# One core: modulation sums issued a step later, and the last attention-output tiles with the router's top 64 by halves of the tokens

## Chip, cores and metric

One NeuronCore of a Trainium2 chip runs the whole program. The metric is the time of one execution on the device in microseconds (us), as the median over several runs. The engines are TensorE (PE, with its weight loads as PEld), VectorE (DVE), ScalarE (ACT), GpSimd (POOL) and SyncE (SP), whose queue issues most of the DMAs.

## What is computed

A hidden state x of 512 tokens by 1024 features goes through two layers (an mLSTM mixer and a short convolution, each followed by an MLP with squared ReLU) and then through a block with modulated norms, two kinds of attention and a mixture of 16 experts. All is float32. Cut to what the change touches:

```python
mod = einsum('bd,de->be', silu(c), w_mod) + b_mod        # 6 x 1024 values, from 1024 inputs
mod_c = einsum('d,de->e', silu(c_ctx), w_mod) + b_mod    # its first 2 x 1024 values are used
...
x = x + g_a * mix                                        # mix = [o_a, o_b] @ w_out
h2 = modulate(rmsnorm(x, norm_ffn), sh_f, sc_f)
x = x + g_f * ec_moe(h2, w_router, w_gate, w_up, w_down)

def ec_moe(h, w_router, w_gate, w_up, w_down):           # 512 tokens, 16 experts
    aff = softmax(einsum('bnd,de->bne', h, w_router), axis=-1)
    vals, idx = top_k(swapaxes(aff, 1, 2), 64)           # each expert takes its 64 best tokens
    # per expert: gather, silu(xs @ w_gate) * (xs @ w_up), @ w_down, times vals, scatter-add
```

## The kernel before

Activations are kept with features on the 128 partitions and tokens along the free dimension: `self.x[:, k]` is feature tile k (of 8), 512 tokens wide. Every GEMM (`gemm`, `mm3`, L92 to L94) is three fp32r matmuls per 128-deep step: high part of the weights with both parts of the activations, and the low part of the weights with their high part. A tile of 128 features by 512 tokens is thus 24 matmuls for a depth of 1024, and 12 for a depth of 512. Weights come as 1 MB pieces through SP's queue (`wpiece`). ACT makes the high half (L85, tag `wh`) and DVE the low half (L86, tag `wl`), two instructions of each per piece; during the MLPs there are four buffers of either, so two pieces.

The compiler orders each engine's instructions itself: the order of the code is their priority, and an instruction that is ready early can stand ahead of an earlier one. `keep_in_program_order` pins an instruction behind the one that precedes it in the code on the same engine. Within an engine instructions start in the order of its queue.

The modulation vector is computed inside the two MLPs by a generator, `mods`, which `mlp` advances (`next(filler)`, L701 and L711) once ahead of each `down(f)` and once behind it. `down(f)` is 8 tiles of 12 matmuls for one of eight blocks of hidden features; the products of a later block (4 tiles of 24, two weight pieces) come between two `down`s. For columns j of `w_mod` (24 blocks of 256) DVE multiplies rows of weights by the silu values and adds them up (L877 first, then L881, tiles `u`, weights `b`). For j under 8 there are two vectors, the token condition and the context's. The first sum of an even j is pinned (L879). `rows` (L842) then sums four such accumulators over the partitions with four matmuls of 32 columns of ones at four column positions of PE, and ACT copies the result (L845). `columns` (L852) transposes it, and DVE copies it to `mod` (L856, L858). In the code, the sums of a pair of blocks and `rows` stand together behind a `down(f)`, and `columns` ahead of the next one.

`attention_out` multiplies the attention result by `w_out`, tile k after tile k. Behind each tile's GEMM stands the router's part of the tile before it (`stats`, L1391): four matmuls with 128 tokens of x as weights and the router's 16 columns moving, eight records in the trace since float32 takes two. DVE updates x (L1409), ACT squares it (L194), and the squares are added on POOL or DVE (L196). Behind the last tile come the column sums of the squares (L207), the reciprocal root (`rstd_cols`, L156 to L162), and the scaled logits (L1415).

`route` computes the softmax (L1424 to L1431) and transposes the affinities to 16 rows of 512 tokens (L1434, L1436). Eight rounds of a maximum of eight (L1460) and a replacement by -1 (L1462) find each expert's top 64. What became negative is selected (L1467, L1469), and matmuls with triangular ones count ranks (L1471, L1473, L1476). Meanwhile PE transposes x to tokens and ACT writes it, scaled, to HBM (`h2d`, L1454 to L1456). One-hot matrices (L1489) give the slots (L1499), and POOL fetches each pair of experts' tokens by an indirect DMA (L1511). `moe` then runs the experts in pairs. The first 15 expert weight tiles are loaded ahead, behind the weights of `attention_out` in SP's queue; later ones wait until their buffers are free.

Of the kernel before, what the change touches and what calls it, by code (L numbers as in the profile page):

```python
# [18 lines left out]
S = 512  # L19
# [8 lines left out]
class Net:  # L28
# [42 lines left out]
    def sm(self, shape, dt=F32):  # L71
        self.n += 1
        return self.smp.tile(shape, dt, name=f"sm{self.n}", tag=f"sm{shape[-1]}", bufs=16 if shape[-1] <= 2 else 2 if shape[-1] == 64 else 8)
# [101 lines left out]
    class Sumsq:  # L175
# [7 lines left out]
        def add(self, src, sl=slice(0, S)):  # L183
# [9 lines left out]
            sq = net.t([128, S]) if lo + 2 == hi else net.t([128, 256], tag="th")  # L193
# [635 lines left out]
    def mods(self):  # L829
# [30 lines left out]
        sums = []  # L860
        for j in range(24):
# [20 lines left out]
            if j % 2:  # L882
                t = None
# [6 lines left out]
                yield  # L890
# [483 lines left out]
    def attention_out(self, oops):  # L1374
# [8 lines left out]
        wa = self.t([128, KD, 16], tag="wr")  # L1383
        nc.gpsimd.tensor_tensor(wa, wr, self.A[:, :, 2][:, :, None].to_broadcast([128, KD, 16]), op=OP.mult)
# [4 lines left out]
        def stats(k):  # L1389
            for c in range(4):  # L1390
                nc.tensor.matmul(pl[:, c * 16:c * 16 + 16], self.x[:, k, c * 128:c * 128 + 128], wa[:, k], start=k + c == 0,  # L1391
                                 stop=k == KD - 1 and c == 3, skip_group_check=True)

        for k in range(KD):
            j = (k + 1) // 2
            if k % 2 == 0 and j + 2 < 5:
# [12 lines left out]
            nc.vector.scalar_tensor_tensor(self.x[:, k], p, self.mod[:, 16 + k, 0:1], self.x[:, k], op0=OP.mult, op1=OP.add)  # L1409
            ss.add(self.x[:, k])  # L1410
        stats(KD - 1)
        cols, _ = self.colsum(ss.acc)
        lg = self.sm([128, 64])
        for c in range(4):
            nc.vector.scalar_tensor_tensor(lg[:, c * 16:c * 16 + 16], pl[:, c * 16:c * 16 + 16], cols[:, c:c + 1], shw,  # L1415
                                           op0=OP.mult, op1=OP.add)
        return cols, lg.rearrange("p (c e) -> p c e", c=4)

    def route(self, cols, lg):
        nc, a = self.nc, self.a  # L1420
        self.tok = self.t([128, S + 4], tag="tok")
        nc.scalar.dma_start(self.tok, a["k_tok"])
        mx = self.sm([128, 4])
        nc.vector.reduce_max(mx, lg, axis=AX.X)  # L1424
        nc.vector.tensor_tensor(lg, lg, mx[:, :, None].to_broadcast([128, 4, 16]), op=OP.subtract)
        nc.scalar.activation(lg, lg, AF.Exp)
        sm = self.sm([128, 4])
        nc.vector.reduce_sum(sm, lg, axis=AX.X)
        ri = self.sm([128, 4])
        nc.vector.reciprocal(ri, sm)  # L1430
        nc.vector.tensor_tensor(lg, lg, ri[:, :, None].to_broadcast([128, 4, 16]), op=OP.mult)  # L1431
        pT = self.p()
        for c in range(4):
            nc.tensor.transpose(pT[0:16, c * 128:(c + 1) * 128], lg[:, c], self.ident)  # L1434
        aT = self.t([16, S], tag="aT")
        nc.vector.tensor_copy(aT, pT[0:16])  # L1436
# [8 lines left out]
        nc.gpsimd.tensor_sub(self.mv[:, :, :, 3:6:2], l4, self.mv[:, :, :, 2:6:2].bitcast(F32))  # L1445

        self.h2d = self.tc.dram_tile([S, D], F32, name="h2d")
        hd = self.h2d.rearrange("(c p) d -> c p d", p=128)
        for c in range(4):
            t = self.t([128, D], tag="wh" if c else "ha")  # L1450
            for hf in range(2):
                p = self.p()
                for j in range(4):
                    nc.tensor.transpose(p[:, j * 128:(j + 1) * 128], self.x[:, hf * 4 + j, c * 128:(c + 1) * 128], self.ident)  # L1454
                nc.scalar.activation(t[:, hf * 512:hf * 512 + 512], p, AF.Copy, scale=cols[:, c:c + 1])
            nc.scalar.dma_start(hd[c], t)  # L1456
        wk = aT
        for r in range(8):
            v = self.sm([16, 8])
            nc.vector.max(v, wk)  # L1460
            nw = self.t([16, S], tag="aT")
            nc.vector.match_replace(out=nw, in_to_replace=v, in_values=wk, imm_value=-1.0)  # L1462
            wk = nw

        pT = self.p()
        for c in range(4):
            nc.tensor.transpose(pT[:, c * 16:c * 16 + 16], wk[:, c * 128:(c + 1) * 128], self.ident[0:16, 0:16])  # L1467
        sel = self.t([128, 4, 16], BF, tag="sel")
        nc.vector.tensor_scalar(sel, pT[:, 0:64].rearrange("p (c e) -> p c e", c=4), 0.0, None, op0=OP.is_lt)  # L1469
        pp = self.p()[:, 0:64].rearrange("p (c e) -> p c e", c=4)  # L1470
        nc.tensor.matmul(pp, tri[:, 0], sel, start=True, stop=False, skip_group_check=True)  # L1471
        for c in range(3):
            nc.tensor.matmul(pp[:, c + 1:], tri[:, 1], sel[:, c:c + 1].to_broadcast([128, 3 - c, 16]), start=False, stop=c == 2,  # L1473
# [315 lines left out]
```

## Time and profile before

| | before |
|---|---|
| median of 3 runs | 1856.34 us (1850.32 to 1859.35) |
| the profiled execution | 1856.87 us |
| its span in the trace | 1854.9 us, mean granted clock 0.975 |
| PE busy | 1753.0 us, 95% (weight loads 1364.1 us, 74%) |
| DVE busy | 1026.3 us, 55% |
| ACT busy | 676.8 us, 36% |
| POOL busy | 150.6 us, 8% |

Times are from the start of the span. Matmul records overlap: each has its full duration though the next starts before it ends, so the distance between starts tells the pace. PEclk is the granted share of TensorE's clock, 1.00 for 2.4 GHz and 0.50 for 1.2 GHz. "[7.52 <-DVE u L881]" behind an instruction is the idle time of its engine ahead of it and what ended it. In the chain of waits, each row is a step of the work that ended last. The timeline leaves out buffer numbers and joins neighbours of one kind ("x8").

### The profile page before, as it was taken

What the parts mean: (1) busy time and instruction counts of PE and PEld (TensorE: products, weight loads), DVE (VectorE), ACT (ScalarE), POOL (GpSimd) and SP (SyncE); (2) the same over time, 40 slices, a digit from 0 to 9 for tenths busy, and PEclk for the clock granted to TensorE, in tenths of its full rate; (3) what the DMA queues carried; (4) which work ended last, traced back from release to release, by engine and by line L of the source; (5) the groups of instructions that cost most, each with busy time, mean ns of one, the idle gap of its engine ahead of it and who ended that gap; (6) DMA issues with size and microseconds to landing.
All of it is one profiled execution on the core that took longest, in us unless ns stands there. A gap on an engine that the chain in (4) does not pass through costs nothing.

```text
span 1854.9 us, 24070 instructions
## 1 busy us (share of the span) xinstructions
PE 1753.0 (95%) x9629; PEld 1364.1 (74%) x9633; DVE 1026.3 (55%) x1953; ACT 676.8 (36%) x1220; POOL 150.6 (8%) x132
## 2 busy tenths in 40 slices
PE   7999999988899999999999999989989998799997
PEld 5798898766687888889787878888777787343334
DVE  4544673456665585537455554578777843342322
ACT  4444444322233253335333333345666642111112
POOL 1000000000000000000000001012334321000000
PEclk9899999988999999999999999989999999899999
DMA  6222423233443423322434432220100048799995
GB/s 191 69 69 65 153 80 114 91 113 114 136 137 114 136 86 97 114 91 92 137 113 137 136 117 91 91 73 12 24 12 9 20 144 305 255 390 393 394 390 185
DMA packets 193535, 254.45 MB, mean 137 GB/s; under 512 B 19975, under 2 KB 125840, under 8 KB 193296
## 3 DMA queue, kind: packets, MB, share of 16 engines
q1 hardware_dynamic: 188688, 244.70, 39.2%
q10 hardware_dynamic: 3232, 3.97, 0.7%
q0 software_dynamic: 1504, 4.26, 0.6%
q8 instruction: 75, 1.23, 0.3%
q14 instruction: 36, 0.29, 0.1%
HBM read 248.71 MB, written 4.19 MB: 136 GB/s over the span
## 4 chain that ended last, share of the span: by engine, by line
PE 84%; DVE 8%; ACT 3%; DMA 3%; issue 1%; POOL 1%; SPq 0%; DVEq 0%; ACTq 0%; POOLq 0%
PE ps L92 21%; PE ps L93 21%; PE ps L94 21%; PE ps L1595 5%; PE ps L1572 3%; PE ps L1187 2%; DMA mw<-in_w_up_dram 2%; PE ps L1172 2%; PE pw L1315 1%; DVE u L881 1%; PE ps L1564 1%; DMA wl<-h2d,slots 1%; DVE wl L86 1%; PE ps L1565 1%; PE ps L842 1%
## 5 line engine op out<-in xcount | busy, mean ns | idle before, releaser
L92 PE MATMUL ps<-op,wh 128*128 128x512 f32 (+1 forms) x1808 | 656.4, 368 | 7.3 <-ACT wh L85 2.3
L93 PE MATMUL ps<-op,wh 128*128 128x512 f32 (+1 forms) x1808 | 659.2, 366 | 0.8 <-DVE op L105 0.6
L94 PE MATMUL ps<-op,wl 128*128 128x512 f32 (+1 forms) x1808 | 657.2, 365 | 2.5 <-DVE wl L86 2.5
L86 DVE TENSOR_TENSOR wl<-raw,wh 128x1024 fp32r<-128x1024 f32 x210 | 258.2, 1233 | 276.9 <-ACT wh L85 276.4
L92 PEld LDWEIGHTS ps<-op,wh 128*128 128x128 f32 x1808 | 339.4, 190 | 71.8 <-issue 4.1
L94 PEld LDWEIGHTS ps<-op,wl 128*128 128x128 f32 x1808 | 342.2, 190 | 64.2 <-DVE wl L86 3.1
L93 PEld LDWEIGHTS ps<-op,wh 128*128 128x128 f32 x1808 | 342.7, 190 | 62.0 <-issue 1.8
L85 ACT CAST wh<-raw 128x1024 fp32r<-128x1024 f32 x210 | 219.9, 1052 | 382.3 <-PE ps L93 346.7
L688 DVE TENSOR_TENSOR t<-t,ps 128x512 f32<-128x512 f32 x96 | 65.8, 685 | 101.7 <-PE ps L94 101.6
L1595 PE MATMUL ps<-mw,xs 128*64 128x512 f32 x400 | 114.2, 607 | 3.1 <-DMA mw<-in_w_up_dram 3.1
L881 DVE SCALAR_TENSOR_TENSOR u<-b,csilu,u 128x256 f32<-128x256 f32 x224 | 103.9, 493 | 9.5 <-DMA b<-in_w_mod_dram 5.8
L196 POOL TENSOR_TENSOR acc<-acc,t 128x512 f32<-128x512 f32 x21 | 28.2, 1342 | 630.3 <-ACT t L194 629.7
L637 ACT ACTIVATE t<-ps 128x512 f32<-128x512 f32 x64 | 38.1, 595 | 107.0 <-PE ps L94 107.0
L1595 PEld LDWEIGHTS ps<-mw,xs 128*64 128x64 f32 x400 | 33.3, 139 | 59.5 <-issue 52.9
L92 PE MATMUL ps<-wh,op 128*128 128x256 f32 x256 | 75.4, 295 | 0.1
L93 PE MATMUL ps<-wl,op 128*128 128x256 f32 x256 | 72.7, 285 | 0.0
L94 PE MATMUL ps<-wh,op 128*128 128x256 f32 x256 | 71.9, 286 | 0.0
L1140 DVE TENSOR_REDUCE sm<-pw 128x1 f32<-128x768 f32 (+2 forms) x64 | 53.9, 854 | 31.5 <-PE pw L1315 18.7
L1557 DVE TENSOR_SCALAR xs<-ps,modA,modc 128x128 f32<-128x128 f32 x32 | 13.0, 409 | 80.6 <-PE ps L1550 73.5
L641 DVE CAST op<-t 128x512 fp32r<-128x512 f32 x64 | 27.1, 424 | 48.9 <-ACT t L639 36.7
L92 PEld LDWEIGHTS ps<-wh,op 128*128 128x128 f32 x256 | 49.2, 192 | 4.2 <-ACT og L532 2.3
L1572 PE MATMUL ps<-mw,t 128*64 128x512 f32 (+1 forms) x184 | 50.9, 543 | 0.0
(459 smaller groups left out, 2244.4 us busy)
## 6 DMA issues: line engine op xcount, KB each, us to landing
raw<-in_w_mlp_up_dram SPq DMA_DIRECT2D x32, 1024.0 KB, 5.4
raw<-in_w_mlp_down_dram SPq DMA_DIRECT2D x32, 1024.0 KB, 5.0
mw<-in_w_gate_dram SPq DMA_DIRECT2D x26, 1024.0 KB, 14.0
b<-in_w_mod_dram SPq DMA_DIRECT2D x48, 512.0 KB, 4.7
mw<-in_w_up_dram SPq DMA_DIRECT2D x24, 1024.0 KB, 14.1
mw<-in_w_down_dram SPq DMA_DIRECT2D x17, 1024.0 KB, 14.3
raw<-in_w_in_conv_dram SPq DMA_DIRECT2D x12, 1024.0 KB, 5.2
raw<-in_w_in_mlstm_dram SPq DMA_DIRECT2D x11, 1024.0 KB, 5.5
```

Source lines behind the costliest of these rows:

```text
L85: nc.scalar.copy(h, raw[:, k0:k0 + kk])
L86: (eng or nc.vector).tensor_sub(lo, raw[:, k0:k0 + kk], h.bitcast(F32))
L92: mm(out, st[0], mv[0], start=first, stop=False)
L93: mm(out, st[0], mv[1], start=False, stop=False)
L94: mm(out, st[1], mv[0], start=False, stop=last)
L637: nc.scalar.activation(t, src, AF.Relu)
L688: nc.vector.tensor_add(y[i], y[i], p)
L881: nc.vector.scalar_tensor_tensor(acc[v], raw[:, k], c, acc[v], op0=OP.mult, op1=OP.add)
L1140: nc.vector.reduce_max(nm[e], p[e][:, 256:256 + n], axis=AX.X, negate=self.sink is None)
L1172: nc.tensor.transpose(pt[:, x * 128:(x + 1) * 128], self.P[e][:, m * 128:(m + 1) * 128], net.ident)
L1572: nc.tensor.matmul(py[e * 64:e * 64 + 64], aT[:, f, e * 64:e * 64 + 64], r[e][:, f], start=f == 0, stop=f == 3, tile_position=(0, e * 64))
L1595: nc.tensor.matmul(p[e * 64:e * 64 + 64], xs[:, k, e * 64:e * 64 + 64], r[e][:, k % 4], start=k == 0, stop=k == 7, tile_position=(0, e * 64))
```

## The change

- `mods`: a `yield` now stands between the sums and `rows`, so `rows` comes one call of `next(filler)` later (ahead of the next `down`), and `columns` with it (behind that `down`, ahead of the next pair's sums). The ones are broadcast from a column, and the copy of `rows` uses tag `t`.
- `attention_out`: tiles 0 to 4 as before; tiles 5 to 7 first for tokens 0 to 255, then for tokens 256 to 511.
- The router's weights are now the stationary operand, padded to 32 columns, with 128 tokens moving; the four token blocks use four column positions of PE. The logits come out transposed and are transposed back per half.
- Root, softmax, affinity transposes and list for half 0 stand among half 1's tiles in the code. Each half finds its own 64 best of 256 tokens (8 maxima, 7 replacements).
- The threshold of an expert is the smallest of the 64 pairwise maxima of one list and the other reversed, which is the 64th best of all. Tokens above it, and equal ones in order of token until 64 are reached, are selected; the ranks count both groups.

```diff
     def mods(self):
-        ones = self.c([128, 32], name="ones32")
-        nc.gpsimd.memset(ones, 1.0)
+        ones = self.ones.to_broadcast([128, 32])
...
-            t = self.t([128, 256], tag="th")
+            t = self.t([128, 256])
...
             if j % 2:
-                t = None
+                yield
                 if len(sums) == 4:
                     t = rows(sums)
                     sums = []
                 yield
                 if t is not None:
                     columns(t, j, nv)
-                yield
+                    t = None
...
     def attention_out(self, oops):
+        wa = self.t([128, KD, 32], tag="op")
+        nc.gpsimd.memset(wa, 0.0)
+        nc.gpsimd.tensor_tensor(wa[:, :, 0:16], wr, ...)
...
+        def stats(k, cs=range(4)):
+            for c in cs:
+                nc.tensor.matmul(pl[32 * c:32 * c + 32, 0:128], wa[:, k], self.x[:, k, c * 128:c * 128 + 128], start=k == 0,
+                                 stop=k == KD - 1, tile_position=(0, 32 * c), skip_group_check=True)
...
-        for k in range(KD):
+        for k in range(5):
...
+        for hf in range(2):
+            sl = self.HALF[hf]
+            for k in range(5, KD):
+                self.gemm(p[:, 0:256], wps[j], slice(c0, c0 + 128), oops, sl=sl)
+                if hf == 0:
+                    stats(k - 1, range(4) if k == 5 else (0, 1))
+                elif k == 5:
+                    stats(KD - 1, (0, 1))
+                    self.rstd_half(0, ss.acc, last[0])
+                else:
+                    stats(k - 1, (2, 3))
+                    if k == 6:
+                        self.softmax_half(0, "op")
+                update(k, p[:, 0:256], sl)
+                if k < KD - 1:
+                    ss.add(self.x[:, k, sl], sl, "op")
+                else:
+                    last[hf] = self.t([128, 256], tag="op")
+                    nc.scalar.activation(last[hf], self.x[:, k, sl], AF.Square)
+        self.affinity_half(0, "op")
+        self.h2d = self.tc.dram_tile([S, D], F32, name="h2d")
+        self.stage_half(0, ("ha", "la"))
+        stats(KD - 1, (2, 3))
+        self.rstd_half(1, ss.acc, last[1])
...
+    def affinity_half(self, hf, tag):
+        pT = self.p()
+        for i in range(2):
+            nc.tensor.transpose(pT[0:16, i * 128:(i + 1) * 128], self.lg[:, 2 * hf + i], self.ident)
+        wk = self.t([16, 256], tag=tag)
+        nc.vector.tensor_copy(wk, pT[0:16, 0:256])
+        top = self.top[hf] = self.sm([16, 64])
+        for r in range(8):
+            v = top[:, 8 * r:8 * r + 8]
+            nc.vector.max(v, wk)
+            if r < 7:
+                nw = self.t([16, 256], tag=tag)
+                nc.vector.match_replace(out=nw, in_to_replace=v, in_values=wk, imm_value=-1.0)
+                wk = nw
...
+    def route(self):
+        self.softmax_half(1, "t")
+        self.affinity_half(1, "aT")
...
+        self.stage_half(1, ("wh", "wh"))
+        m = self.top[0]
+        nc.vector.tensor_tensor(m, m, self.top[1][:, ::-1], op=OP.max)
+        th = self.sm([16, 1])
+        nc.vector.tensor_reduce(th, m, axis=AX.X, op=OP.min)
+        nc.tensor.transpose(pT[:, 0:16], th.to_broadcast([16, 128]), self.ident[0:16, 0:16])
+        nc.vector.tensor_tensor(sel[:, :, 0], lg, T, op=OP.is_gt)
+        nc.vector.tensor_tensor(sel[:, :, 1], lg, T, op=OP.is_equal)
...
+        for c in range(4):
+            nc.tensor.matmul(pp[:, :, 1], tri[:, 1], sel[:, c:c + 1, 0].to_broadcast([128, 4, 16]), start=False, stop=c == 3,
+                             skip_group_check=True)
+        both = self.t([128, 4, 2, 16])
+        nc.vector.tensor_mul(both, pp, sel)
+        nc.vector.tensor_add(rank, both[:, :, 0], both[:, :, 1])
```

`rstd_half`, `softmax_half` and `stage_half` hold, for two blocks of 128 tokens, the steps that `attention_out` and `route` had for four: column sums (the last tile's squares as a second matmul in place of an addition), root, scaled logits (after a copy and a transpose), softmax, and the transposes of x, scaling and writing of `h2d`.

## Rows read from the trace of the kernel before

**Rows 1.** List of waits: who waited for whom, us, times, longest us.
```profile
PE ps L842 <- DVE u L881: 22.6, 3, 7.5
```
**Rows 2.** Timeline of PE at the first wait: start us, us, instruction, [idle before].
```profile
371.27 0.39 PE L94 MATMUL ps<-op,wl 128*128 128x512 f32 x1
...
379.18 1.06 PE L842 MATMUL ps<-u,ones 128*32 128x256 f32 x4 [7.52 <-DVE u L881]
...
385.39 0.40 PE L94 MATMUL ps<-op,wl 128*128 128x512 f32 x1
```
**Rows 3.** Windows: us, busy (instructions) of PE, PEld, DVE, ACT, POOL, PEclk, DMA, GB/s.
```profile
380.00:384.00 4.00, 4.00 (x10) 2.08 (x9) 4.00 (x9) 0.00 (x0) 0.00 (x0) 0.50 0.87 270
```
**Rows 4.** Timeline of PE at the two other waits, last and ninth matmul.
```profile
428.31 0.40 PE L94 MATMUL ps<-op,wl 128*128 128x512 f32 x1
...
442.84 0.39 PE L94 MATMUL ps<-op,wl 128*128 128x512 f32 x1
...
485.75 0.39 PE L94 MATMUL ps<-op,wl 128*128 128x512 f32 x1
...
499.08 0.40 PE L94 MATMUL ps<-op,wl 128*128 128x512 f32 x1
```
**Rows 5.** Timeline of PE where the sums' matmuls do not wait.
```profile
325.49 0.39 PE L94 MATMUL ps<-op,wl 128*128 128x512 f32 x1
325.80 0.64 PE L842 MATMUL ps<-u,ones 128*32 128x256 f32 x8
326.37 0.50 PE L92 MATMUL ps<-op,wh 128*128 128x512 f32 x1
```
**Rows 6.** Timeline of DVE around the first wait.
```profile
361.69 1.22 DVE L86 TENSOR_TENSOR wl<-raw,wh 128x1024 fp32r<-128x1024 f32 x1
...
377.07 5.62 DVE L881 SCALAR_TENSOR_TENSOR u<-b,csilu,u 128x256 f32<-128x256 f32 x14
382.61 1.21 DVE L86 TENSOR_TENSOR wl<-raw,wh 128x1024 fp32r<-128x1024 f32 x1
...
384.12 3.61 DVE L881 SCALAR_TENSOR_TENSOR u<-b,csilu,u 128x256 f32<-128x256 f32 x7
```
**Rows 7.** Timeline of PE: the column transposes ahead of a down tile.
```profile
348.88 0.38 PE L852 MATMUL ps<-ident,th 128*128 128x128 f32 x2
```
**Rows 8.** Timeline of PE in the last attention-output tile.
```profile
1554.36 0.96 PE L1391 MATMUL ps<-wr,xres 128*128 128x16 f32 x8
1555.16 0.48 PE L92 MATMUL ps<-op,wh 128*128 128x512 f32 x1
1555.49 0.39 PE L93 MATMUL ps<-op,wh 128*128 128x512 f32 x1
...
1560.61 0.39 PE L94 MATMUL ps<-op,wl 128*128 128x512 f32 x1
```
**Rows 9.** Timeline of PE: GEMM matmuls of 256 columns, in an MLP's last step.
```profile
1214.45 0.28 PE L94 MATMUL ps<-op,wl 128*128 128x256 f32 x1
1214.57 0.28 PE L92 MATMUL ps<-op,wh 128*128 128x256 f32 x1
```
**Rows 10.** The chain of waits behind the attention output: start us, us, step.
```profile
1563.29 1.07 PE ps L207 x8
...
1565.70 0.67 DVE sm L1415 x4
...
1567.94 1.03 PE ps L1434 x4
...
1569.72 0.69 DVE sm L1460
1570.43 0.75 DVE aT L1462 x2
...
1580.88 0.75 DVE aT L1462 x2
...
1583.28 0.43 DVE oh L1489
```

More of the change, by code (lines that the diff above doesn't have):

```diff
@@ L72, in sm @@
         self.n += 1
[L73 removed]
+        return self.smp.tile(shape, dt, name=f"sm{self.n}", tag=f"sm{shape[-1]}", bufs=16 if shape[-1] <= 2 else 3 if shape[-1] == 64 else 8)
     def wpiece(self, src, k, n, tags=("wh", "wl"), eng=None, raw=None):
@@ L1387, in attention_out, with update @@
         ss = self.Sumsq(self)
[L1389 to L1392, printed above, removed]
-        for k in range(KD):
+        def stats(k, cs=range(4)):
+            for c in cs:
+                nc.tensor.matmul(pl[32 * c:32 * c + 32, 0:128], wa[:, k], self.x[:, k, c * 128:c * 128 + 128], start=k == 0,
+                                 stop=k == KD - 1, tile_position=(0, 32 * c), skip_group_check=True)
+        def update(k, p, sl):
+            xk = self.x[:, k, sl]
+            nc.vector.scalar_tensor_tensor(xk, p, self.mod[:, 16 + k, 0:1], xk, op0=OP.mult, op1=OP.add)
+        for k in range(5):
             j = (k + 1) // 2
-            if k % 2 == 0 and j + 2 < 5:
+            if k % 2 == 0:
                 wps.append(piece(j + 2))
@@ L1408, in attention_out @@
                 stats(k - 1)
-            nc.vector.scalar_tensor_tensor(self.x[:, k], p, self.mod[:, 16 + k, 0:1], self.x[:, k], op0=OP.mult, op1=OP.add)
+            update(k, p, slice(0, S))
             ss.add(self.x[:, k])
[L1411 to L1415, printed above, removed]
-                                           op0=OP.mult, op1=OP.add)
@@ new lines, in attention_out, with rstd_half @@
+        self.affinity_half(0, "op")
[3 more added lines that the diff above has]
+        self.rstd_half(1, ss.acc, last[1])
+    def rstd_half(self, hf, acc, last):
+        nc = self.nc
+        pc = self.p()
+        for i in range(2):
+            c = 2 * hf + i
+            nc.tensor.matmul(pc[:, i:i + 1], acc[:, c * 128:(c + 1) * 128], self.ones, start=True, stop=False)
+            nc.tensor.matmul(pc[:, i:i + 1], last[:, i * 128:(i + 1) * 128], self.ones, start=False, stop=True)
+        y = self.rstd_cols(pc[:, 0:2], 2, 1.0 / D)
+        nc.vector.tensor_copy(self.cols[:, 2 * hf:2 * hf + 2], y)
@@ new lines, in softmax_half @@
+    def softmax_half(self, hf, tag):
+        nc = self.nc
+        lT = self.t([128, 128], tag=tag)
+        sp = slice(64 * hf, 64 * hf + 64)
+        nc.scalar.copy(lT[sp], self.pl[sp, 0:128])
+        pt = self.p()
+        nc.tensor.transpose(pt[:, 0:64], lT[sp], self.ident[sp, sp])
+        lg = self.lg[:, 2 * hf:2 * hf + 2]
+        for i in range(2):
+            nc.vector.scalar_tensor_tensor(lg[:, i], pt[:, 32 * i:32 * i + 16], self.cols[:, 2 * hf + i:2 * hf + i + 1], self.shw,
+                                           op0=OP.mult, op1=OP.add)
+        mx = self.sm([128, 2])
+        nc.vector.reduce_max(mx, lg, axis=AX.X)
+        nc.vector.tensor_tensor(lg, lg, mx[:, :, None].to_broadcast([128, 2, 16]), op=OP.subtract)
+        nc.scalar.activation(lg, lg, AF.Exp)
+        sm = self.sm([128, 2])
+        nc.vector.reduce_sum(sm, lg, axis=AX.X)
+        ri = self.sm([128, 2])
+        nc.vector.reciprocal(ri, sm)
+        nc.vector.tensor_tensor(lg, lg, ri[:, :, None].to_broadcast([128, 2, 16]), op=OP.mult)
@@ new lines, in affinity_half @@
+    def affinity_half(self, hf, tag):
+        nc = self.nc
+        pT = self.p()
+        for i in range(2):
+            nc.tensor.transpose(pT[0:16, i * 128:(i + 1) * 128], self.lg[:, 2 * hf + i], self.ident)
[9 more added lines that the diff above has]
+                wk = nw
@@ new lines, in stage_half @@
+    def stage_half(self, hf, tags):
+        nc = self.nc
+        hd = self.h2d.rearrange("(c p) d -> c p d", p=128)
+        for i in range(2):
+            c = 2 * hf + i
+            t = self.t([128, D], tag=tags[i])
+            for h in range(2):
+                p = self.p()
+                for j in range(4):
+                    nc.tensor.transpose(p[:, j * 128:(j + 1) * 128], self.x[:, h * 4 + j, c * 128:(c + 1) * 128], self.ident)
+                nc.scalar.activation(t[:, h * 512:h * 512 + 512], p, AF.Copy, scale=self.cols[:, c:c + 1])
+            nc.scalar.dma_start(hd[c], t)
@@ L1445, in route @@
         nc.gpsimd.tensor_sub(self.mv[:, :, :, 3:6:2], l4, self.mv[:, :, :, 2:6:2].bitcast(F32))
[L1447 to L1463, printed above, removed]
-        pT = self.p()
[L1466 to L1469, printed above, removed]
```

46 lines of the change are left out of this document (20 added, 26 removed).

## The prediction

> **What bounds the kernel now.** I read the page first: the matrix engine (PE) is busy for nearly the whole span, so only stretches where PE stands still, or runs at its lower clock, are worth looking for. The list of waits comes next. Among PE's own waits one line stands out: L842, the matmuls of the modulation sums, waits for VectorE's L881, 22.6 us in 3 waits of up to 7.5 us [rows 1]. The timeline shows the first of them [rows 2]: the last matmul of a down tile starts at 371.27, the next work is L842 at 379.18, and the ninth GEMM matmul behind the gap starts at 385.39. The usual cadence is (1560.61 - 1555.49) / 22 = 0.233 us for a 512-column matmul [rows 8], so without a wait it would start at 371.27 + 9 x 0.233 = 373.37. 12.0 us are lost, more than the idle 7.5, because PE comes back slow: the granted share is 0.50 from 380 to 384 [rows 3], the 1.2 GHz level, after PE had stood idle. The two other waits, counted in the same way [rows 4], lose 442.84 - 428.31 - 2.10 = 12.4 and 499.08 - 485.75 - 2.10 = 11.2 us. Together that is 35.7 us.
>
> The second place is the end of the attention output. PE runs its GEMM without a gap to 1560.61 + 0.23 = 1560.84, and then the chain of waits leads through small steps to the one-hot matrices at 1583.28 [rows 10]. Of these 22.4 us, eight rounds of a maximum and a replacement on VectorE take 1580.88 + 0.75 - 1569.72 = 11.9.
>
> **Part 1, the modulation sums later.** Nothing is added, and only a memset of ones is dropped. The four L842 matmuls move behind the next four product tiles (96 GEMM matmuls, 22.4 us), and the column transposes L852 move with them by a step. This takes the three waits away if PE has other work at 371.50. The product tiles behind the gap use their weights in pieces of two L86 results each, and four `wl` buffers hold two pieces. The first piece's second half was made at 361.69; the second piece's second half comes at 382.61 [rows 6], its first half just before the sums. So 48 matmuls (first piece, two tiles) and 12 more (half of the third tile) can run at once: 60 x 0.233 = 14.0 us, to 385.5. The third matmul after these is the first to need the result of 382.61 + 1.21 = 383.8. Ahead of the first sum, which is pinned to the order of the code, now stand two column copies of 4 elements, for which I allow 0.4 us: 384.2 against 371.50 + 62 x 0.233 = 386.0. VectorE is what would be late next, and has 1.8 us in hand; so the wait goes nowhere.
>
> What stays is the cost of the sums' own matmuls. Where they do not wait, they take 326.37 - 325.49 less one cadence, 0.65 us [rows 5]. Saved: 35.7 - 3 x 0.65 = 33.7 us. The other five groups of L842 make no wait on PE and cost the same wherever they stand. The queues passed: ScalarE's copy L845 follows its matmuls, and nothing wants it until the columns, a step later; SyncE's loads of `b` wait for sums that do not move; two of the four `u` buffers are held 22 us longer; the copy takes one of 16 `t` buffers in place of a `th`. I price these at nothing: the 1.8 us in hand hides them, and without it each microsecond costs three.
>
> **Part 2, the last tiles by halves.** Three tiles of 24 matmuls become six of 24 with 256 columns; such a matmul takes 0.12 us start to start [rows 9], half of 0.233: no change. The router call takes 0.80 us of PE now (1554.36 to 1555.16) [rows 8], and six stand ahead of the last matmul: 4.8 us. Its new form is not in the trace. The nearest is L842, also four 128x32 weights side by side, with 256 columns, 0.65 us, of which four passes of 0.117 stream; with 128 columns 0.65 - 0.23 = 0.42 (ends 0.2 and 0.65). Five full and four half calls, the column groups running together, cost 9 x 0.42 = 3.8. New in the stream are half 0's column sums, eight records against today's eight in 1.07 [rows 10], and a transpose of 0.3. So the last matmul moves by -4.8 + 3.8 + 1.4 = +0.4 us (-1.6 to +2.5).
>
> Then the chain. A list operation on 256 elements is not in the trace. On 512 a maximum takes 1570.43 - 1569.72 = 0.71 and a round 11.9 / 8 = 1.49, so a replacement 0.78 [rows 10]. L881, on 256 elements, starts every 5.62 / 14 = 0.40 us [rows 6], which speaks for an operation half streaming, half fixed: I take 0.44 and 0.52 (ends: half, 0.36 and 0.39, and nothing off). A half's list of 8 maxima and 7 replacements then takes 7.2 us (5.6 to 11.1); both take 14.4 against 11.9. Half 0's list can start only behind its softmax, which follows half 0's column sums and half 1's second tile; I place its first maximum 1.3 us behind the last matmul, at 1562.5, so it lies behind the GEMM. Half 1's root (1.3 from 1564.36 to 1565.70) and softmax (2.2 from there to 1567.94) run beside it if VectorE alternates them, else after it. Alternating: 1562.5 + 7.2 + 2.6 (these small operations without their waits) + 1.3 (transposes and copy, 1.8 now for four blocks) + 7.2 + 3.0 (join, threshold and four more matmuls, against 1.65 now) = 1583.8; in series 1584.7. Against 1583.28 that is +0.5 to +1.4; -2.7 with the cheapest list operations, +8 with the dearest. I take +0.5, the price nearest to the 256-element row. Staging half 0 early moves ScalarE work that no one waited for.
>
> **The sum.** The profiled execution took 1856.87 us (span 1854.9): 1856.9 - 33.7 + 0.5 = 1823.7. The median shown is 0.5 below that execution: **1823 us**. The stages behind are shifted whole: the expert weights of the first rounds are loaded ahead, and further loads wait for the first expert matmuls to free buffers.
>
> **Rivals.**
> A. The weights become late. If the L86 of 382.61 comes behind all sums, also the eight that VectorE makes ahead for the next step (3.6 us from 384.12 [rows 6]), PE waits 3.6 - 1.8 = 1.8 us, and more with other shifts, in three places, and may fall to the lower clock: 5 to 20 us given back, 1828 to 1843, middle 1836. For it speaks the small 1.8 us; against it the queue in the trace, where L86 stands ahead of those eight.
> B. The matmuls do not move in PE's queue, since the order within a queue is the compiler's: 1856.3 + 0.5, 1857. For: queues in the trace differ from the code. Against: the sums used at 325.80 [rows 5] still stood behind the whole tile that precedes them in the code.
> C. Slower: the pin. A step's first sum now waits behind the column copies, and these for PE's transposes. If PE takes the transposes behind the product tiles, VectorE stands still and the weights with it. It decides from 33.7 / 3 + 1.8 = 13 us of standing a step; at the 22.4 us of a whole product stage it costs 3 x (22.4 - 1.8) - 33.7 = +28: 1885. Against: the transposes at 348.88 [rows 7] came right behind the tile ahead of them in the code.
> D. The router's column groups run one after another. Four passes of 0.06 for each of four groups are 0.94 us, with the fixed 0.18 and eight loads of about 0.1 not hidden 1.1 to 1.9 a call; seven call equivalents 8 to 13 against 3.8: about 1830. Against: the eight L842 matmuls take 0.64 us together [rows 5], where 16 passes of 0.117 in series would take 1.9. The Trainium skill (TensorE: Matmul & The Clock Gate, Part 3: Packing small matmuls — row/col tiling) says that weight loads overlap running matmuls only where the row group differs, and column tiles share their rows; by that rule D would come about, and this trace does not agree with it for L842.
> E. The lists are cheaper or start under the GEMM: -4 or more, 1818 or less.
>
> **Chances.** Forecast 0.64 (1818 to 1828), A 0.18, B 0.06, C 0.05, D 0.03, E 0.04. The range 1817 to 1838 takes in the forecast, D, E's near end and over half of A: about 0.8. Half a per cent, 9.3 us, is about what a measurement here can tell from no change: faster 0.64 + 0.18 + 0.03 + 0.04 = 0.89, same 0.06 (B), slower 0.05 (C).
>
> **What would show it.** After the change: no wait of L842 for L881 in the list of waits; the granted clock at its upper level through 370 to 500; L842 behind four product tiles. If PE's L94 waits for L86 instead, it is A. At the end: router calls near 0.4 us, list operations near 0.44 and 0.52, and 20 to 24 us from the last GEMM matmul to the one-hots. If that chain shrinks by over 3 us, my price of a list operation or its start is wrong; if PE idles elsewhere in the first MLP for over 5 us, the 1.8 us in hand were misread.

## The result, and the profile after

| | before | after |
|---|---|---|
| median (4 runs each) | 1855.21 us (1850.32 to 1859.35) | 1828.30 us (1827.85 to 1829.14) |
| ratio, 95% interval | | 0.9856 (0.9831 to 0.9882) |
| the profiled execution | 1856.87 us | 1828.06 us |
| its span, mean granted clock | 1854.9 us, 0.975 | 1826.3 us, 0.983 |

The change saves 27 us (22 to 31). The prediction said 1823, 33 us under the 1856.3 that it started from: the time lies in its range, some 5 us above the forecast, and 6 us of the saving are missing (the median of before came out 1 us lower). From one profiled execution to the other the span falls by 28.6.

**The first place did what was forecast.** The list of waits of the changed kernel, PE's own part (who waited for whom, us, times, longest us), has no wait of the sums' matmuls (L841 now) for the sums any more; the longest rows are others. PE's waits for the low halves of the weights (L86), the sign of rival A, are what they were in before (2.5 us in three). This answers [rows 1].

```profile
PE ps L1487 <- DVE sm L1480: 7.4, 1, 7.4
PE ps L1626 <- DMA wl<-h2d,slots: 5.7, 2, 4.8
PE ps L207 <- DVE acc L319: 5.2, 2, 3.4
...
PE ps L94 <- DVE wl L86: 2.4, 3, 1.6
```

In PE's timeline the sums' matmuls stand four product tiles behind the column transposes, with no idle time ahead of them, and the window that was at the lower clock in [rows 3] is at the upper one, as is all of 370 to 500 (granted share 1.00; 0.89 in before):

```profile
369.31 0.38 PE L851 MATMUL ps<-ident,t 128*128 128x128 f32 x2
...
392.11 0.64 PE L841 MATMUL ps<-u,ones 128*32 128x256 f32 x8
```
```profile
380.00:384.00 4.00, 4.00 (x18) 3.22 (x18) 3.72 (x7) 2.18 (x3) 0.00 (x0) 1.00 0.86 278
```

Counted by GEMM matmuls (the n-th of one trace against the n-th of the other), PE gains 11.7, 12.1 and 10.9 us where the three waits were, and gives back 0.63 at each place to which the matmuls moved. This is the forecast, to within 1 us. But all along the way something else takes a little back.

**The second place got longer.** The chain of waits behind the attention output, to be read against [rows 8] and [rows 10]: the router call takes 0.35 (0.80 before), and from start to start a maximum takes 0.45 and a replacement 0.51 (0.71 and 0.78 before).

```profile
1505.69 0.35 PE ps L1392 x8
1506.04 0.32 PE ps L92
...
1541.55 0.43 DVE sm L1493
1542.00 0.48 DVE aT L1496 x2
1542.51 0.43 DVE sm L1493
...
1551.27 0.43 DVE oh L1565
```

The last GEMM matmul starts at 1527.18, and one step of such a matmul (0.12) behind that the chain begins: 24.0 us to the one-hot matrices, where 22.4 passed before. (An expectation below has 24.3: it takes the end of the GEMM 0.35 us too early.)

```profile
1527.18 0.28 PE L94 MATMUL ps<-op,wl 128*128 128x256 f32 x1
```

**Two things were not in the prediction.** Behind the one-hots the kernel takes 1826.29 - 1551.27 = 275.0 us to its end, before 1854.89 - 1583.28 = 271.6. The list of waits from 1560 on has PE waiting 6.9 us for expert weights, in before 3.1:

```profile
PE ps L1671 <- DMA mw<-in_w_up_dram: 4.0, 3, 1.6
PE ps L1671 <- DMA raw<-in_w_up_dram: 1.7, 1, 1.7
...
PE ps L1648 <- DMA mw<-in_w_down_dram: 1.2, 2, 1.0
```

And the step from one 512-column matmul of the GEMMs (L92 to L94) to the next, averaged over all pairs that follow each other directly, is 0.2342 us where it was 0.2333, at the same full granted clock (within the MLPs alone 0.2343 and 0.2333). The changed kernel has 3966 such matmuls, which makes 3.6 us, and 2664 of 256 columns, whose step grows by about as much, from 0.1175 to 0.1186: 2.9 us more. So it is some 6 us if PE sets the pace throughout (an estimate).

### The profile page after: what moved, and what is told of

The parts are those of the page before. It is cut to its first block, busy times and chain, and to the rows that moved or that the text cites. A ratio compares the mean times of both kernels' runs of the same rounds, so it can differ in the third digit from the quotient of the medians.

```text
span 1826.3 us, 24308 instructions
## 1 busy us (share of the span) xinstructions
PE 1742.3 (95%) x9712; PEld 1361.2 (75%) x9716; DVE 1030.0 (56%) x1994; ACT 678.4 (37%) x1228; POOL 149.3 (8%) x131
## 3 DMA queue, kind: packets, MB, share of 16 engines
q8 instruction: 76, 1.25, 0.3%
## 4 chain that ended last, share of the span: by engine, by line
PE 83%; DVE 7%; DMA 5%; ACT 3%; issue 1%; POOL 1%; SPq 0%; DVEq 0%; ACTq 0%; POOLq 0%
PE ps L92 21%; PE ps L94 21%; PE ps L93 21%; PE ps L1671 5%; PE ps L1648 3%; PE ps L1186 2%; PE ps L1171 2%; DMA mw<-in_w_up_dram 2%; PE pw L1314 1%; DMA raw<-in_w_up_dram 1%; DVE u L880 1%; PE ps L1640 1%; PE ps L1641 1%; DMA wl<-h2d,slots 1%; DVE wl L86 1%
## 5 line engine op out<-in xcount | busy, mean ns | idle before, releaser
L92 PE MATMUL ps<-op,wh 128*128 128x512 f32 (+1 forms) x1832 | 659.9, 365 | 7.2 <-ACT wh L85 2.7
L94 PE MATMUL ps<-op,wl 128*128 128x512 f32 (+1 forms) x1832 | 660.9, 362 | 2.4 <-DVE wl L86 2.4
L86 DVE TENSOR_TENSOR wl<-raw,wh 128x1024 fp32r<-128x1024 f32 x210 | 258.1, 1233 | 258.8 <-ACT wh L85 258.2
L92 PEld LDWEIGHTS ps<-op,wh 128*128 128x128 f32 x1832 | 343.1, 189 | 71.2 <-issue 4.7
L94 PEld LDWEIGHTS ps<-op,wl 128*128 128x128 f32 x1832 | 346.3, 189 | 61.2 <-DVE wl L86 3.1
L93 PEld LDWEIGHTS ps<-op,wh 128*128 128x128 f32 x1832 | 346.5, 189 | 59.1 <-DVE op L309 1.0
L92 PE MATMUL ps<-wh,op 128*128 128x256 f32 x256 | 75.0, 294 | 0.1
L94 PE MATMUL ps<-wh,op 128*128 128x256 f32 x256 | 71.5, 284 | 0.0
L92 PEld LDWEIGHTS ps<-wh,op 128*128 128x128 f32 x256 | 48.3, 189 | 4.1 <-ACT og L532 2.3
L93 PEld LDWEIGHTS ps<-wl,op 128*128 128x128 f32 x256 | 48.5, 189 | 0.2
```

The costliest lines, as they stand in the source:

```text
L86: (eng or nc.vector).tensor_sub(lo, raw[:, k0:k0 + kk], h.bitcast(F32))
L92: mm(out, st[0], mv[0], start=first, stop=False)
L93: mm(out, st[0], mv[1], start=False, stop=False)
L94: mm(out, st[1], mv[0], start=False, stop=last)
```

## The experiments

Kernels of one part below ran beside each other on one chip, with the kernel before among them. Twelve more executions of the unchanged code, as a kernel of its own, gave a ratio to its like of 0.9987 (0.9977 to 0.9998): differences of 0.2% (3 us) between two kernels are not settled by their medians, and there I read stretches of the traces. The groups of runs came from different chips, so across them the ratios, each to the kernel before on the same chip, count for more than the medians.

### The kernel before once more, the change once more

No edit in either.

> The kernel before once more, with its own trace, beside the next three on one chip. The changed kernel's trace shows 0.2343 us from one 512-column matmul to the next where the trace of before shows 0.2333, both at the full granted clock. If the pace belongs to the execution and not to the kernel, this trace shows either pace with unchanged code, and the ratio to before is 1.000 within 0.003. If the change slows the matmuls, this trace shows 0.2333 and the changed kernel beside it 0.2343.

Measured: 1853.55 us (before beside it 1855.35). Its trace has the step of 0.2333 us. So the pace belongs to the code, not to an execution.

> The changed kernel once more. Forecast of the prediction: 33.2 us under before; first measurement: 27 us under. Theory: the modulation part gives its 32 to 34 us, the part by halves costs 2 to 6, so 27 to 31 us under. In the expert stage the trace again shows PE waiting for weights (some 3.5 us of them between 1675 and 1720) if that belongs to the change; if it belonged to that one execution, the expert stage is as long as in the kernel before.

Measured: 1828.13 us, 0.9853 (0.9831 to 0.9874); the step is 0.2342, the waits for expert weights are there again, and from the one-hots to the end it takes 275.3 us. All three things belong to the change.

### The modulation sums alone, the halves alone

The first is the part of the diff in `mods`; the second is the rest, with the ones broadcast as well.

> Only the first part: sums' matmuls one step later, the attention output and routing as before. By the prediction's count 33.7 us under before. Rival (the shortfall lies in this part: the expert stage or other weights give time back): 27 us or less under. No wait of the sums' matmuls for VectorE in the list of waits; matmul cadence as in the other runs of this chip.

Measured: 1828.26 us, 0.9845 (0.9829 to 0.9860), which is 28.8 us under before, by as much as the whole change. There is no wait of the sums' matmuls, but the step is 0.2342 us here too, and it takes 274.4 us from the one-hots to the end, though this kernel's routing and experts are the code of before.

> Only the second part: the last three tiles by halves, the router with its weights stationary and the lists joined by a threshold; modulation sums in their old order (their ones come from a broadcast column, for lack of room). By the prediction +0.5 us (-2.7 to +8) against before. Theory after the first result: +2 to +6, of which 1.9 in the chain from the last GEMM matmul to the one-hot matrices (24.3 us there, against 22.4). Rival: 0 or below, and the shortfall is in the first part.

Measured: 1862.54 us, 1.0039 (1.0024 to 1.0054), 7 us slower, with a step of 0.2342. So both parts alone have the slower pace. What they share is that the tile of ones is dropped:

```diff
-        ones = self.c([128, 32], name="ones32")
-        nc.gpsimd.memset(ones, 1.0)
+        ones = self.ones.to_broadcast([128, 32])
```

The tile takes 128 bytes per partition, and everything that is allocated behind it moves down by that. In the program of before the activation tiles (tag `op`, which PE reads in every GEMM) start at multiples of 512 bytes. With the sums' edit alone they lie 384 above one; in the whole change and in the halves, where one more buffer of 256 bytes was added, 128 above one. The tiles of the MLPs' weights (`wh`, `wl`) did not move. These are the addresses that the build gives.

### Putting the tiles back

The first part with an unused tile where the ones were, the changed kernel with the same and one small buffer fewer (the second half's list lies in a `t` buffer), before without its ones, and before with a small buffer of 256 bytes fewer:

```diff
         ones = self.ones.to_broadcast([128, 32])
+        pad = self.c([128, 32], name="pad32")
+        nc.gpsimd.memset(pad, 0.0)
```

> The first part alone, and beside it an unused tile of 128 bytes per partition in place of the dropped tile of ones. In the three changed kernels measured so far a 512-column matmul follows the last at 0.2343 us, in both traces of before at 0.2333; what these kernels have in common is that the dropped tile of ones (and one more small buffer) moves the activation tiles (tag op) from a multiple of 512 bytes to 384 or 128 above one. If the address makes the pace, this kernel runs at 0.2333 and gives 33 to 36 us under before (1820 to 1822). Rival (the broadcast of the ones, or the order of the program, makes the pace): 0.2343 and 27 to 29 us under, as without the pad. In the expert stage the weights streamed at 387 GB/s in the changed kernels, at 392 in before: by an address as cause 392 again, else 387.

Measured: 1821.41 us, 0.9820 (0.9805 to 0.9834). The step is 0.2333 again.

> The kernel before with nothing changed but the tile of ones (128 bytes per partition), dropped for a broadcast column; activation tiles then lie 384 bytes above a multiple of 512. Address theory: pace 0.2343, some 5900 steps of 512 columns by 0.001 = 5.5 to 6 us more than before, with perhaps 2 to 3 more from the expert weights. Rival: no change.

Measured: 1860.09 us, 1.0029 (1.0017 to 1.0041), 5.4 us slower than before with no other edit; the step is 0.2341.

> The kernel before with one buffer of 64 columns fewer among the small tiles, so that the activation tiles move by 256 bytes, to 256 above a multiple of 512; the rest is as before. If a multiple of 256 is enough for the pace: 0.2333 and no change in time. If it takes 512: 0.2343 and 5 to 9 us more.

Measured: 1854.15 us, 0.9997 (0.9986 to 1.0007), step 0.2333. An address 256 bytes above a multiple of 512 costs nothing; 128 and 384 above it cost the step 1 ns.

> The changed kernel with the activation tiles back on a multiple of 512 bytes (the second half's list lies in a t buffer and not in a third small one of 64 columns, and an unused tile of 128 bytes stands where the ones stood). Address theory: pace 0.2333, 5.7 us less than the changed kernel, with the expert weights back at 392 GB/s 7 to 9 less: 1819 to 1822, and by that the prediction's 1823 came from terms that hold. Rival: 1828 as without it.

Measured: 1823.18 us, 0.9830 (0.9815 to 0.9844), step 0.2333, and 272.5 us from the one-hots to the end.

The pace can be seen in PE's timeline, in one stretch of 96 GEMM matmuls and two transposes, from the last matmul of a down tile to the last ahead of the sums. First the kernel with the sums alone (tiles at 384), then with the pad (at 0):

```profile
370.28 0.39 PE L94 MATMUL ps<-op,wl 128*128 128x512 f32 x1
370.51 0.38 PE L851 MATMUL ps<-ident,t 128*128 128x128 f32 x2
...
392.98 0.39 PE L94 MATMUL ps<-op,wl 128*128 128x512 f32 x1
393.31 0.64 PE L841 MATMUL ps<-u,ones 128*32 128x256 f32 x8
```
```profile
368.69 0.39 PE L94 MATMUL ps<-op,wl 128*128 128x512 f32 x1
368.92 0.38 PE L853 MATMUL ps<-ident,t 128*128 128x128 f32 x2
...
391.31 0.40 PE L94 MATMUL ps<-op,wl 128*128 128x512 f32 x1
391.64 0.64 PE L843 MATMUL ps<-u,ones 128*32 128x256 f32 x8
```

392.98 - 370.28 = 22.70 against 391.31 - 368.69 = 22.62: 0.08 us in 96 matmuls, and nowhere a wait. Counted matmul by matmul, the kernel without the pad falls behind the one with it by 1.2 us up to 280 and by 4.9 up to 1100, some 0.4 us in each 100.

Two things more stand in these traces. The loss is by the matmul and not by the column: 256 columns lose as much as 512. And it is not the moving operand alone: in one early GEMM (L519) the weights move, from the same addresses in every program, and the activations are the stationary operand, and there too the step of 256 columns goes from 0.1183 to 0.1199 when the activation tiles lie 128 or 384 above a multiple of 512.

The expert weights follow the same pattern; windows of the stage in which they stream (last column GB/s), the sums alone, the same with the pad, before without ones, and before at 256:

```profile
1640.00:1720.00 80.00, 74.05 (x319) 27.84 (x316) 22.77 (x45) 11.89 (x22) 1.87 (x2) 1.00 1.05 388
```
```profile
1640.00:1720.00 80.00, 75.47 (x326) 28.90 (x322) 25.40 (x49) 11.52 (x21) 1.87 (x2) 1.00 1.05 392
```
```profile
1640.00:1720.00 80.00, 77.48 (x351) 30.47 (x348) 25.76 (x51) 12.48 (x23) 1.88 (x2) 1.00 1.05 387
```
```profile
1640.00:1720.00 80.00, 77.47 (x350) 30.39 (x350) 25.91 (x50) 12.48 (x23) 1.88 (x2) 1.00 1.05 392
```

The transfers go at 392 GB/s with the tiles on a multiple of 256 bytes, at 387 or 388 else, with the same DMA share (1.05). Of the 14 buffers that these weights use in turn, 12 (`mw` and `raw`) have one address in all these programs, 224 bytes above a multiple of 256; the other two (`mz`, side by side) start at byte 38400 or 38144 where the rate is 392, and at 38272 or 38528 where it is lower. The Trainium skill (DMA: Bandwidth & Descriptors, How a descriptor splits into AXI transactions) says of reads that a transaction has to start on a 256-byte boundary, so that a descriptor which does not start on one fetches bytes that it has no use for. Here the buffers are written, which the section does not speak of; for these two the runs agree in sign. That they are the cause was not separated from the other tiles that moved.

### How thick was the cover of the first part?

The sums with the pad, and ahead of the pinned first sum eight additions that no result needs, where there are two vectors:

```diff
                         if hf + k == 0:
+                            if v == 0 and j < 8 and j % 2 == 0:
+                                for _ in range(8):
+                                    self.tc.keep_in_program_order(nc.vector.tensor_add(pair, raw[:, 0:2], raw[:, 2:4]))
                             o = nc.vector.tensor_scalar(acc[v], raw[:, k], c, None, op0=OP.mult)
```

> The first part alone with the activation tiles on their multiple of 512 bytes (1821.4 us), and ahead of each pinned first sum of the steps with two vectors eight additions of 512 columns on VectorE, some 4.9 us a step, that no result needs. In the trace without them the low half of the second product piece is made at 381.72 and PE first needs it at 383.61: 1.9 us in hand (the prediction said 1.8). So PE should wait for L86 some 3 us in three places, 9 us in all, and up to 13 with a lower clock: 1830 to 1834. Rival (the compiler puts L86 ahead of the additions, or the cover is thicker than read): 1821 to 1823.

Measured: 1822.14 us, 0.9820 (0.9805 to 0.9835), within the noise of the kernel without the additions. VectorE's timeline shows the low half 8.5 us later than without them (380.50 there), so the load was real:

```profile
389.03 1.23 DVE L86 TENSOR_TENSOR wl<-raw,wh 128x1024 fp32r<-128x1024 f32 x1
```

PE needed it at 383.61, but PE did not wait. Its queue had been built in another order:

```profile
387.63 0.62 PE L843 MATMUL ps<-u,ones 128*32 128x256 f32 x4
389.32 0.62 PE L843 MATMUL ps<-u,ones 128*32 128x256 f32 x2
390.30 0.62 PE L843 MATMUL ps<-u,ones 128*32 128x256 f32 x2
```

The sums' matmuls, in three groups as the sums end, and before them the first half of the fourth product tile, whose weights were there, stand ahead of the matmuls that need the late weights (the first of them starts at 392.11). By the count of GEMM matmuls against the kernel without the additions, each of the three steps loses 1.46 us, 4.4 together: what PE pays is two more groups of the sums' matmuls, at 0.64 to 0.75 each, and no wait. My expectation of 9 to 13 was wrong: the compiler made another order of PE's queue for the larger load, so the delay was not passed on microsecond by microsecond.

This run also tests rival A. Here the low half came behind all 32 of VectorE's sums, also the eight for the next step (without the additions it stood ahead of those eight), which is the case that A priced at 5 to 20 us of PE waiting; PE did not wait for it.

### The second part taken apart

First only the router with its weights stationary, on top of the sums with the pad; then the padded change with the first half's work moved forward; then with VectorE's comparison for the triangular ones behind the threshold.

```diff
-                nc.tensor.matmul(pl[:, c * 16:c * 16 + 16], self.x[:, k, c * 128:c * 128 + 128], wa[:, k], ...)
+                nc.tensor.matmul(pl[32 * c:32 * c + 32, 0:128], wa[:, k], self.x[:, k, c * 128:c * 128 + 128], ...,
+                                 tile_position=(0, 32 * c))
...
+        lT = self.t([128, 128], tag="op")
+        nc.scalar.copy(lT, pl[:, 0:128])
+        pt = self.p()
+        nc.tensor.transpose(pt[:, 0:128], lT, self.ident)
```

> The first part with the activation tiles on their multiple of 512 bytes (1821.4 us), and of the second part only the router with its weights stationary, over all 512 tokens; one list of 512, no halves, no join. The router call takes 0.35 us of PE in the changed kernel's trace against 0.80, seven of them ahead of the last matmul of the GEMM; the copy and transpose of the logits lie beside the column sums and the root. Expected: 3 us less than the first part alone, 1818 to 1819. Rival: the transposition ends behind the root and eats it, 1821.

Measured: 1820.28 us, 0.9804 (0.9791 to 0.9818), 1.1 below the sums alone by the medians and 3.0 by the ratios. The trace is clearer: from the first router call to the end of the GEMM 36.83 us against 38.97, so 2.1 less, and 22.5 from there to the one-hots as before (22.4). The stationary router is a gain on its own, though a third smaller than I expected.

```diff
                     self.rstd_half(0, ss.acc, last[0])
+                    self.softmax_half(0, "op")
                 else:
                     stats(k - 1, (2, 3))
                     if k == 6:
-                        self.softmax_half(0, "op")
+                        self.affinity_half(0, "op", range(0))    # transposes and copy
                 update(k, p[:, 0:256], sl)
                 if k < KD - 1:
                     ss.add(self.x[:, k, sl], sl, "op")
+                    if hf and k == 6:
+                        self.affinity_half(0, "op", range(4))    # four rounds
...
-        self.affinity_half(0, "op")
...
         stats(KD - 1, (2, 3))
         self.rstd_half(1, ss.acc, last[1])
+        self.softmax_half(1, "op")
+        self.affinity_half(0, "op", range(4, 8))
+        self.stage_half(0, ("ha", "la"))
```

> The changed kernel with its activation tiles on their multiple of 512 bytes (1823.2 us), and the first half's softmax one tile earlier, its transposes ahead of the last tile, four rounds of its list there, the second half's root and softmax ahead of the other four. In the changed kernel's trace the first half's affinities were ready at 1526.42, but their transposes stood behind the whole GEMM and its list began at 1528.60; the second half's root, ready on ScalarE at 1532.07, stood behind that list until 1537.03. Theory (the order in the queues costs, not the list): first list from about 1525, the chain behind the GEMM 5 to 7 us shorter, 1816 to 1818. Rival (VectorE's total work bounds the chain, or the GEMM is held up by the transposes): 1822 or more.

Measured: 1817.73 us, 0.9804 (0.9791 to 0.9817), 5.5 below the padded change by the medians, 4.8 by the ratios. By the traces it is 3.5: 2.0 from the first router call to the one-hots (61.87 against 63.88) and 1.5 behind them; the rest lies ahead of the first router call, where the two codes are the same. The first list starts at 1520.31, ahead of the end of the GEMM (1522.46); the one-hots come at 1544.57. But only part of what the earlier list should have given arrives there, and VectorE's timeline shows what is in the way:

```profile
1532.24 0.40 DVE L1503 MATCH_REPLACE8 aT<-t,aT 16x256 f32<-16x256 f32 x1
1536.52 0.35 DVE L1529 TENSOR_SCALAR tri<-tok 128x128 bf16<-128x128 f32 x1 [3.88 <-DMA tok<-in_k_tok_dram]
1536.79 0.41 DVE L1500 MAX8 t<-aT 16x8 f32<-16x256 f32 x1
```

```diff
-        nc.vector.tensor_scalar(tri[:, 0], self.tok[:, 0:128], self.tok[:, S:S + 1], None, op0=OP.is_ge)
...
         nc.vector.tensor_reduce(th, m, axis=AX.X, op=OP.min)
+        self.tc.keep_in_program_order(
+            nc.vector.tensor_scalar(tri[:, 0], self.tok[:, 0:128], self.tok[:, S:S + 1], None, op0=OP.is_ge))
```

> As the kernel with the first half early (1817.7 us), and the comparison that makes the triangular ones pinned on VectorE behind the threshold, so that VectorE doesn't meet the token table's transfer in the middle of the second list. In the trace without it VectorE stood 3.88 us there (to 1536.52) with five rounds of the list queued behind. Theory: that wait was the bound, 3.5 to 4 us less, 1813 to 1815, and 18 us from the last GEMM matmul to the one-hot matrices, against 22.1. Rival (the second half's staging or the table on other engines is late next): 1817 or more.

Measured: 1815.56 us, 0.9792 (0.9778 to 0.9805), the fastest of all. From the last GEMM matmul to the one-hots it takes 18.0 us, 4.1 less, as expected; the time itself lies between what I expected (1813 to 1815) and the rival's 1817:

```profile
1538.73 0.27 DVE L1542 TENSOR_SCALAR tri<-tok 128x128 bf16<-128x128 f32 x1
...
1540.91 1.77 DVE L1573 TENSOR_TENSOR oh<-tok,rank 128x256 fp32r<-128x256 f32 x5
```

Of these 4.1 us 2.2 reach the end by the medians, 3.1 from span to span. What is late next stands in its chain of waits: the writes of the staged tokens, which land at 1543.5, just as the first fetch wants them.

```profile
1527.22 8.11 DMA h2d<-ha
1535.37 0.04 issue
1535.40 8.08 DMA h2d<-wh
```

## Why the prediction was right, and where it was not

**Part 1 was right in its mechanism and its size.** The forecast was 33.7 us; with the tiles back in place the sums alone give 33.4 (30.8 to 36.2). Each term holds: no wait is left, PE stays at its upper clock, and the four matmuls cost 0.63 where they now stand (forecast 0.65). The cover was read well: with the pad, the low half that is late next is made from 380.50 to 381.72, and the first matmul that needs it starts at 383.61, 1.9 us later (forecast 1.8). Rivals A, B and C did not come about. The time alone would not tell: 1828.3 lies at the upper edge of the forecast's own 1818 to 1828 and in A's 1828 to 1843. The list of waits does, with 2.4 us for L86 against 2.5 in before.

```profile
380.50 1.22 DVE L86 TENSOR_TENSOR wl<-raw,wh 128x1024 fp32r<-128x1024 f32 x1
```

What was wrong is what I said of that cover, "without it each microsecond costs three": eight additions, 4.8 us a step, cost 1.46 a step, 4.4 in all, where 3 x (4.8 - 1.9) = 9 was to be expected, since PE's queue was ordered anew.

**The step that failed is the one priced at nothing:** "Nothing is added, and only a memset of ones is dropped." The memset is worth nothing, but its tile held 128 bytes, and dropping it moved the activation tiles off their boundary. That costs 5.4 us (3.2 to 7.6) in the kernel before by itself, and putting the tiles back takes 1828.1 - 1823.2 = 5 us from the change (4.3 by the ratios, whose intervals overlap) and 4.6 by the ratios from the sums alone. The change with its tiles in place takes the 1823 that was forecast, so the 5 us above it are this one term. That it meets the forecast to 0.2 us is luck: it saves 31.8 us of 1855.0, and the forecast was 33.2 of 1856.3; the start was taken 1.3 us too high, and part 2 came out 1.3 dearer.

The same term broke "the stages behind are shifted whole": from the one-hots to the end the time is 270.9 to 272.5 us in all nine traces with the tiles in place (on a multiple of 256 bytes), 273.2 to 275.3 in the five without. The expert stage streams its weights all the time [the window of 1640 to 1720], and at 388 GB/s in place of 392 PE waits for them 6.9 us in the change and 4.9 in the padded one, 2.0 of the 2.5 us between the two.

**Part 2 was right in its sign, and 1 to 2 us too low.** Forecast +0.5 (-2.7 to +8); the padded change against the sums with the pad is +1.8 by the medians and +2.5 by the stretch from the first router call to the one-hots (63.88 against 61.40, one trace each; other traces of the unchanged code with PE at its upper clock have up to 62.4). Step by step:

- The last GEMM matmul: forecast +0.4, measured 39.99 - 38.97 = +1.0. The call itself was priced rightly: by the measure of the 0.42, from start to start less a cadence, it takes 0.44 (0.35 from the end of the matmul ahead to its own end). So rival D is out: the column groups do run together. The rule of the Trainium skill (TensorE: Matmul & The Clock Gate, Part 3: Packing small matmuls — row/col tiling) that the prediction set beside D is on weight loads, that they overlap running matmuls only where the row group differs. This trace does not agree with it, as L842 did not: the second four loads of a call start 0.03 us behind its first four matmuls, which take 0.30. What I left out is the matmul behind a call. It ends 0.32 behind the call in a tile of 256 columns, where 0.117 is the cadence, and 0.43 in one of 512, where 0.233 is, so 0.2 more, nine times; in before it was 0.33 against 0.233, so 0.1, six times. Counted from end to end that makes 9 x (0.35 + 0.2) - 6 x (0.80 + 0.1) = -0.4 where I had 3.8 - 4.8 = -1.0, which is the difference of 0.6.
- The list operations: forecast 0.44 and 0.52, measured 0.45 and 0.51; a half's list forecast 7.2, the second one took from 1541.55 to the next step at 1548.71, 7.2. This step held, and the first maximum came 1528.60 - 1527.30 = 1.3 behind the last matmul's end (forecast 1.3).
- From the first maximum to the one-hots: forecast 1583.8 - 1562.5 = 21.3, measured 1551.27 - 1528.60 = 22.7. The terms that I did not have are two waits in VectorE's queue. In the first list it stood 1.25 us for the second half's column sums. And the second half's softmax stood behind the comparison for the triangular ones, which waited 0.92 us for the table `tok` and took 0.35, while in before that transfer was hidden. Of these 2.5 us, 1.1 came back, most of it in the small operations and the joining of the lists, which took less than I allowed.

```profile
1531.23 0.16 DVE L156 TENSOR_SCALAR sm<-ps 128x2 f32<-128x2 f32 x1 [1.25 <-PE ps L1456]
...
1538.59 0.19 DVE L1477 TENSOR_REDUCE sm<-sm 128x2 f32<-128x32 f32 x1 [0.29 <-ACT sm L1475]
1539.69 0.35 DVE L1522 TENSOR_SCALAR tri<-tok 128x128 bf16<-128x128 f32 x1 [0.92 <-DMA tok<-in_k_tok_dram]
1539.96 0.15 DVE L1479 RECIPROCAL sm<-sm 128x2 f32<-128x2 f32 x1
```

Rival E, lists under the GEMM, did not come about in the change, but not for want of time: half 0's transposes were placed behind the whole GEMM by the order of the code. The early version shows that it is possible, and that, with the stationary router and the pinned comparison, it turns the second part from +1.8 us into a gain: 5 to 6 by medians and ratios (1815.56 us and 0.9792, against 1821.41 and 0.9820, on two chips), 4.2 by the traces from the first router call to the end.

What stays open: whether it is those two buffers alone that slow the weights' transfers, and why 128 bytes matter to PE at all. Offsets of 0, 128, 256 and 384 bytes were measured, and no others.

## What to carry to other kernels

An edit that only drops or adds a small buffer moves everything behind it, and a saving that is short by a few tenths of a per cent everywhere, without a wait to show for it, is a reason to compare the pace of one plain matmul in both traces. A wait is best sought in the queue and not in the engine's load: the two gains at the end came from moving a few instructions that stood ahead of ready work. And a reserve read from one trace is that of one order of the queues; the compiler makes another when the load changes.

## What the runs showed of the hardware

- A 512-column matmul (f32, moving tiles in rows of 2048 bytes) follows the last at 0.2333 us when the moving tile lies 0 or 256 bytes above a multiple of 512, and at 0.2343 when it lies 128 or 384 above one; both at the full granted clock (means within the MLPs). 256 columns lose as much (0.1175 to 0.1186), and so they do where the activation tile is the stationary operand (0.1183 to 0.1199).
- Expert weights streamed at 392 GB/s in the programs of the first case and at 387 to 388 in those of the second.
- Four matmuls with 32 columns of weights each, at four column positions and with 128 columns moving, take 0.35 us together, from the end of the matmul ahead to their own; two of them at two positions take 0.34. The full-width matmul behind them ends 0.2 us later than its cadence.
- A maximum of eight over 16 x 256 takes 0.45 us from start to start and a replacement 0.51, against 0.71 and 0.78 over 16 x 512: halving the columns takes off some 36%, not half.
